# Binary cross entropy over 8192 x 8192: two large slots with split targets instead of three smaller ones with one target slot

## The chip, the cores and the metric

The kernel runs on one core of one Trainium2 chip. The metric is the device time of one execution in microseconds (us), lower is better; the median of the runs is compared. A profile is one further execution of the same program with the hardware profiler on.

## The reference

```python
def setup_inputs():
    return {
        "pred": np.random.uniform(0.01, 0.99, (8192, 8192)).astype(np.float32),
        "target": np.random.randint(0, 2, (8192, 8192)).astype(np.float32),
    }

def reference(pred, target):
    eps = 1e-7
    pred = np.clip(pred, eps, 1 - eps)
    return -(target * np.log(pred) + (1 - target) * np.log(1 - pred))
```

Targets are 0 or 1, so the result of an element is -ln(|(t - 1) + p|) with the clipped p: for t = 1 the logarithm's argument is p, for t = 0 it is 1 - p. The kernel computes it in this form. Two float32 arrays of 268.4 MB are read and one is written.

## The kernel before

The arrays are taken as one flat run of elements, cut into **chunks**. A chunk of width w takes 128 x w consecutive elements, and partition r gets row r of w elements, so a transfer has 128 rows of one contiguous run each. `plan` (lines 17 to 24) makes the list: two chunks of width FIRST (5120), then 35 of width BIG (14336), two of LAST (5632) and one of TAIL (1024), 40 in all. They are numbered k = 0 to 39; the big ones are 2 to 36, and a, b, c are the last three (37, 38, 39).

Two tiles hold everything. `ring_p` (line 53) is float32 and has SLOTS = 3 slots of BIG columns and a strip of TAIL columns for c. Predictions land in a slot, all steps work in place, and the result is stored from the same slot; chunk k of the big ones takes slot (k - 1) % 3. `ring_t` (line 54) is bfloat16 and has **one** slot of BIG columns and the strip; targets are cast from float32 to bfloat16 by the transfer that loads them.

The steps of a chunk, each a helper:

- `load_t(k)` (line 75) and `load_p(k)` (line 72) are issued by GpSimd (POOL); only chunk 0's predictions come from ScalarE's queue (line 70), as two transfers of 64 rows.
- `clip` (line 88) on VectorE (DVE): max and min with the two bounds.
- `log` is three instructions: on DVE (t - 1) + p (line 94), then on ScalarE (ACT) `Abs` (line 97) and `Ln` (line 98).
- `back` (line 102) on DVE multiplies by -1.
- `store(k)` (line 79) is issued by POOL; from k = n - 3 = 37 on by SyncE (SP). `store_rows` (line 84) stores c as three transfers on SP.

The order is written out by hand (lines 104 to 158): each engine takes its instructions in the order in which they stand there, and an instruction that waits holds up all behind it on its engine. The waits follow from the tiles: a load into a slot waits until what was there has been read, a step waits for the step before it on the same columns.

A big chunk is computed in two halves (the `h` loop, line 123): clip and log of half 0, clip and log of half 1, then back of both. On POOL's queue the order around big chunk k is `load_t(k+1)`, `store(k)`, `load_p(k+2)`. As there is one target slot, `load_t(k+1)` waits until line 94 has read the second half of chunk k's targets. `load_p(k+2)` goes into the slot of chunk k - 1 and waits for that chunk's store. In the last big chunk (the `else` at line 128) the loads of a, b and c are issued instead, and the clips of a and b stand between the two halves' backs. At the end (lines 145 to 158) DVE's order is log of both halves of a, clip of c, log of b's first half, back of a's first half, and so on, with the stores of a, b and c on SP as they come ready.

Of the kernel before, what the change touches and what calls it, by code (L numbers as in the profile page):

```python
# [1 line left out]

# [4 lines left out]

EPS = 1e-7

BIG = 14 * 1024  # L10
FIRST = 5 * 1024
LAST = 5632
TAIL = 1024
SLOTS = 3


def plan(total):
    n = (total - 2 * FIRST - 2 * LAST - TAIL) // BIG
    assert n > 4 and total == 2 * FIRST + n * BIG + 2 * LAST + TAIL
    spots = [(FIRST, 0, 0), (FIRST, FIRST, FIRST)]  # L20
    spots += [(BIG, k % SLOTS * BIG, 0) for k in range(1, n + 1)]
    end = (n + 1) % SLOTS * BIG
    spots += [(LAST, end, 0), (LAST, end + LAST, LAST)]
    return spots + [(TAIL, SLOTS * BIG, BIG)]


@with_exitstack
def kernel(
    ctx: ExitStack,
    tc: tile.TileContext,  # L30
    pred: bass.AP,
    target: bass.AP,
    out: bass.AP,
):
    nc = tc.nc
    fp32 = mybir.dt.float32
    bf16 = mybir.dt.bfloat16
    Alu = mybir.AluOpType
    Act = mybir.ActivationFunctionType
    P = nc.NUM_PARTITIONS  # L40

    R, C = pred.shape
    spots = plan(R * C // P)
    n = len(spots)
    widths = [s[0] for s in spots]
    cols = [sum(widths[:k]) for k in range(n)]

    def chunk(ap, k):
        flat = ap.rearrange("r c -> (r c)")
        return flat[cols[k] * P : (cols[k] + widths[k]) * P].rearrange("(p w) -> p w", p=P)  # L50

    pool = ctx.enter_context(tc.tile_pool(name="rings", bufs=1))
    ring_p = pool.tile([P, SLOTS * BIG + TAIL], fp32, name="ring_p", tag="ring_p")
    ring_t = pool.tile([P, BIG + TAIL], bf16, name="ring_t", tag="ring_t")
    warm = pool.tile([1, 8], fp32, name="warm", tag="warm")

    def spot(k, part=(0, 1)):
        w, c, _ = spots[k]
        i, m = part
        return ring_p[:, c + i * w // m : c + (i + 1) * w // m]  # L60

    def spot_t(k, part=(0, 1)):
        w, _, c = spots[k]
        i, m = part
        return ring_t[:, c + i * w // m : c + (i + 1) * w // m]

    def load_p(k):
        if k == 0:
            for rows in (slice(0, P, 2), slice(1, P, 2)):
                nc.scalar.dma_start(out=spot(0)[rows], in_=chunk(pred, 0)[rows])  # L70
        else:
            nc.gpsimd.dma_start(out=spot(k), in_=chunk(pred, k))  # L72

    def load_t(k):
        nc.gpsimd.dma_start(out=spot_t(k), in_=chunk(target, k))  # L75

    def store(k):
        queue = nc.sync if k >= n - 3 else nc.gpsimd
        queue.dma_start(out=chunk(out, k), in_=spot(k))  # L79

    def store_rows(k):
        src, dst = spot(k), chunk(out, k)
        for first, last in ((0, 108), (108, 120), (120, 128)):
            nc.sync.dma_start(out=dst[first:last], in_=src[first:last])

    def clip(k, *part):
        p = spot(k, *part)
        nc.vector.tensor_scalar(  # L88
            out=p, in0=p, scalar1=EPS, scalar2=1 - EPS, op0=Alu.max, op1=Alu.min
        )  # L90

    def log(k, *part):
        p = spot(k, *part)
        nc.vector.scalar_tensor_tensor(  # L94
            out=p, in0=spot_t(k, *part), scalar=1.0, in1=p, op0=Alu.subtract, op1=Alu.add
        )
        nc.scalar.activation(out=p, in_=p, func=Act.Abs)  # L97
        nc.scalar.activation(out=p, in_=p, func=Act.Ln)  # L98

    def back(k, *part):  # L100
        p = spot(k, *part)
        nc.vector.tensor_scalar(out=p, in0=p, scalar1=-1.0, scalar2=None, op0=Alu.mult)  # L102

    with tc.manual_schedule():
        nc.vector.memset(warm, 1.0)  # L105
        load_t(0)
        load_p(0)
        load_t(1)
        load_p(1)
        load_p(2)  # L110
        nc.scalar.activation(out=warm, in_=warm, func=Act.Ln)  # L111
        for k in (0, 1):
            clip(k)
            log(k)
        load_t(2)
        back(0)
        store(0)
        back(1)
        store(1)
        load_p(3)  # L120
        a, b, c = range(n - 3, n)
        for k in range(2, n - 3):
            for h in (0, 1):
                clip(k, (h, 2))
                log(k, (h, 2))
            if k < n - 4:
                load_t(k + 1)
            else:
                load_t(a)
                load_t(b)  # L130
                load_p(c)
                load_t(c)
                back(k, (0, 2))
                for j in (a, b):
                    clip(j)
            if k < n - 4:
                back(k, (0, 2))
            back(k, (1, 2))
            store(k)
            if k + 2 < n - 3:  # L140
                load_p(k + 2)
            elif k + 2 == n - 3:
                load_p(a)
                load_p(b)
        log(a, (0, 2))
        log(a, (1, 2))
        clip(c)
        log(b, (0, 2))
        back(a, (0, 2))
        log(b, (1, 2))  # L150
        back(a, (1, 2))
        store(a)
        log(c)
        back(b, (0, 2))
        back(b, (1, 2))
        store(b)
        back(c)
        store_rows(c)


# [1 line left out]
_INS = ['pred', 'target']  # L162
_OUTS = [((8192, 8192), 'float32')]


# [23 lines left out]
```

## Time and profile before

| what | value |
|---|---|
| time, median of 3 runs | 1864.76 us (1864.24 to 1865.12) |
| span of the profiled execution | 1863.3 us |
| the runs' median less that span | 1.5 us |
| DVE busy | 1121.6 us (60%), 230 instructions |
| ACT busy | 902.4 us (48%), 156 instructions |
| POOL busy | 178.7 us (10%), 120 instructions |
| DVE idle ahead of line 94, until a target load landed | 370.7 us in 35 waits |
| POOL idle ahead of line 75, until line 94 was done | 1056.4 us in 37 waits |
| POOL idle ahead of line 79, until line 102 was done | 584.2 us |
| transfers of big chunks, us from issue to landing | predictions 44.3, targets 31.3, stores 31.1 |

The profiled execution's own time outside the profile isn't recorded; the runs' median lies 1.5 us above its span, and that is taken for what lies around a span. The page divides the span into 40 slices; its DMA row is the mean busy share of the core's 16 DMA engines in tenths. The GB/s row counts bytes as they land, so that a target load that reads 4 bytes and writes 2 counts half of what it reads. Idle time of an engine that isn't the bottleneck costs nothing.

### The profile page before, as it was taken

Reading aid. Unit: us, or ns where it says so; the run is one execution under the profiler, and the core shown is the slowest. Engines: PE = TensorE matmul, PEld = TensorE weight load, DVE = VectorE, ACT = ScalarE, POOL = GpSimd, SP = SyncE. Lnnn points to the kernel's source line nnn. Section 1 sums busy time; section 2 is a strip of 40 time slices with the busy share of each in tenths; the row PEclk is TensorE's granted clock in tenths of the full one; section 3 lists DMA queues with packets and bytes.
Section 4 is the critical chain, followed back from the end, with each engine's and each line's share of the span. In section 5 each row is a group of like instructions: output and inputs, shape, how many; then the busy total and the mean of one; then the engine's idle time right before and its main releaser. Section 6 shows DMA issues by size and latency. Waiting matters only on the chain.

```text
span 1863.3 us, 713 instructions
## 1 busy us (share of the span) xinstructions
DVE 1121.6 (60%) x230; ACT 902.4 (48%) x156; POOL 178.7 (10%) x120
## 2 busy tenths in 40 slices
DVE  4666555555666566655555666566655555666565
ACT  4454444455555544444445555544444445555554
POOL 1111101111110011101111110011101111110020
DMA  9999999999999999999999999999999999999999
GB/s 344 348 370 356 355 356 355 355 355 355 357 375 374 374 372 355 355 355 355 355 355 355 359 374 374 375 375 361 355 355 356 356 356 355 356 367 374 374 353 352
DMA packets 17318, 671.15 MB, mean 360 GB/s; under 512 B 1952, under 2 KB 1952, under 8 KB 2336
## 3 DMA queue, kind: packets, MB, share of 16 engines
q0 software_dynamic: 16704, 662.18, 99.0%
q1 hardware_dynamic: 448, 6.29, 0.8%
q10 hardware_dynamic: 160, 2.62, 0.4%
q14 instruction: 6, 0.05, 0.0%
HBM read 536.87 MB, written 268.44 MB: 432 GB/s over the span
## 4 chain that ended last, share of the span: by engine, by line
DMA 60%; issue 35%; ACT 3%; DVE 1%; POOL 0%; POOLq 0%; DVEq 0%; PEldq 0%
DMA ring_t<-in_target_dram 58%; DMA ring_p<-in_pred_dram 2%; ACT ring_p L98 1%; ACT ring_p L97 1%; DVE ring_p L94 1%; DVE ring_p L102 0%; POOL out_dram L79 0%; DVE ring_p L88 0%; POOL ring_t L75 0%; POOLq L75 0%; POOL ring_p L72 0%; POOLq L79 0%; DVEq L94 0%; PEldq L184 0%
## 5 line engine op out<-in xcount | busy, mean ns | idle before, releaser
L97 ACT ACTIVATE ring_p<-ring_p 128x7168 f32<-128x7168 f32 (+3 forms) x77 | 452.0, 5870 | 940.7 <-DVE ring_p L94 940.7
L94 DVE SCALAR_TENSOR_TENSOR ring_p<-ring_t,ring_p 128x7168 f32<-128x7168 bf16 (+3 forms) x77 | 558.2, 7251 | 372.0 <-DMA ring_t<-in_target_dram 370.7
L102 DVE TENSOR_SCALAR ring_p<-ring_p 128x7168 f32<-128x7168 f32 (+3 forms) x77 | 285.4, 3707 | 329.4 <-ACT ring_p L98 329.4
L98 ACT ACTIVATE ring_p<-ring_p 128x7168 f32<-128x7168 f32 (+3 forms) x77 | 452.6, 5877 | 2.4
L88 DVE TENSOR_SCALAR ring_p<-ring_p 128x7168 f32<-128x7168 f32 (+3 forms) x75 | 284.6, 3794 | 24.4 <-DMA ring_p<-in_pred_dram 24.4
L79 POOL DMA_DIRECT2D out_dram<-ring_p x37 | 128.0, 3459 | 584.4 <-DVE ring_p L102 584.2
L75 POOL DMA_DIRECT2D ring_t<-in_target_dram x40 | 29.0, 724 | 1057.2 <-DVE ring_p L94 1056.4
L72 POOL DMA_DIRECT2D ring_p<-in_pred_dram x39 | 21.8, 561 | 2.5 <-issue 2.5
L111 ACT ACT_TABLE_LOAD x1 | 1.3, 1283 | 1.9 <-issue 1.9
L105 DVE MEMSET warm<- 1x8 f32 x1 | 0.1, 65 | 0.8 <-PEq L173 0.8
L111 ACT ACTIVATE warm<-warm 1x8 f32<-1x8 f32 x1 | 0.2, 208 | 0.0
L173 POOL MEMSET const-float32-0.0<- 128x1 f32 x1 | 0.1, 99 | 0.2 <-issue 0.2
L173 POOL MEMSET const-bfloat16-1.0<- 128x1 bf16 x1 | 0.1, 102 | 0.0
L173 POOL MEMSET const-uint8-127<- 128x1 uint8 x1 | 0.1, 100 | 0.0
L173 POOL MEMSET const-float32-1.0<- 128x1 f32 x1 | 0.1, 99 | 0.0
## 6 DMA issues: line engine op xcount, KB each, us to landing
ring_p<-in_pred_dram POOLq DMA_DIRECT2D x35, 7168.0 KB, 44.3
out_dram<-ring_p POOLq DMA_DIRECT2D x35, 7168.0 KB, 31.1
ring_t<-in_target_dram POOLq DMA_DIRECT2D x35, 3584.0 KB, 31.3
ring_p<-in_pred_dram POOLq DMA_DIRECT2D x2, 2816.0 KB, 37.1
out_dram<-ring_p SPq DMA_DIRECT2D x2, 2816.0 KB, 14.6
out_dram<-ring_p POOLq DMA_DIRECT2D x2, 2560.0 KB, 27.9
ring_t<-in_target_dram POOLq DMA_DIRECT2D x2, 1408.0 KB, 26.5
ring_p<-in_pred_dram ACTq DMA_DIRECT2D x2, 1280.0 KB, 10.5
```

The lines of the kernel that those rows point to most:

```text
L72: nc.gpsimd.dma_start(out=spot(k), in_=chunk(pred, k))
L75: nc.gpsimd.dma_start(out=spot_t(k), in_=chunk(target, k))
L79: queue.dma_start(out=chunk(out, k), in_=spot(k))
L88: nc.vector.tensor_scalar(out=p, in0=p, scalar1=EPS, scalar2=1 - EPS, op0=Alu.max, op1=Alu.min)
L94: nc.vector.scalar_tensor_tensor(out=p, in0=spot_t(k, *part), scalar=1.0, in1=p, op0=Alu.subtract, op1=Alu.add)
L97: nc.scalar.activation(out=p, in_=p, func=Act.Abs)
L98: nc.scalar.activation(out=p, in_=p, func=Act.Ln)
L102: nc.vector.tensor_scalar(out=p, in0=p, scalar1=-1.0, scalar2=None, op0=Alu.mult)
L105: nc.vector.memset(warm, 1.0)
L111: nc.scalar.activation(out=warm, in_=warm, func=Act.Ln)
L173: nc = _bacc.Bacc("TRN2", target_bir_lowering=False, num_devices=1)
```

## The change

Widths and slots: BIG goes from 14336 to 16384 columns (a row of a transfer has 64 KiB instead of 56), FIRST from 5120 to 3072, LAST from 5632 to 4608. There are two prediction slots instead of three, and `ring_t` gets two slots of its own, at the same column offsets as `ring_p`. The plan has then 36 chunks: 0 and 1 of 3072, 31 big ones (2 to 32), a and b (33, 34) of 4608 and c (35) of 1024. Big chunk k takes slot (k - 1) % 2 in both rings; a and b share slot 0.

Order: the loads of chunk k + 1 are issued ahead of the computing of chunk k, targets first. On POOL's queue it is then `store(k-1)`, `load_t(k+1)`, `load_p(k+1)`, `store(k)`. `load_p(k+1)` goes into the slot that `store(k-1)` reads and waits for its end. In the last big chunk the three target loads and then the three prediction loads of a, b and c are issued there. `load_t(2)` is issued at the start.

Pieces: a big chunk is computed in eight pieces of 2048 columns: clip and log of all eight, then back of all eight, then the one store.

End: the clips of a, b and c all stand ahead of the logs of a. Stores go to SP from k = n - 4 on, so that the last big chunk's store is issued there too.

```diff
-BIG = 14 * 1024
-FIRST = 5 * 1024
-LAST = 5632
+BIG = 16 * 1024
+FIRST = 3072
+LAST = 4608
 TAIL = 1024
-SLOTS = 3
+SLOTS = 2
+PIECES = 8
...
-    spots += [(BIG, k % SLOTS * BIG, 0) for k in range(1, n + 1)]
+    spots += [(BIG, k % SLOTS * BIG, k % SLOTS * BIG) for k in range(1, n + 1)]
     end = (n + 1) % SLOTS * BIG
-    spots += [(LAST, end, 0), (LAST, end + LAST, LAST)]
-    return spots + [(TAIL, SLOTS * BIG, BIG)]
+    spots += [(LAST, end, end), (LAST, end + LAST, end + LAST)]
+    return spots + [(TAIL, SLOTS * BIG, SLOTS * BIG)]
...
-    ring_t = pool.tile([P, BIG + TAIL], bf16, name="ring_t", tag="ring_t")
+    ring_t = pool.tile([P, SLOTS * BIG + TAIL], bf16, name="ring_t", tag="ring_t")
...
-        queue = nc.sync if k >= n - 3 else nc.gpsimd
+        queue = nc.sync if k >= n - 4 else nc.gpsimd
...
         load_t(1)
-        load_p(1)
-        load_p(2)
+        for k in (1, 2):
+            load_p(k)
+        load_t(2)
         nc.scalar.activation(out=warm, in_=warm, func=Act.Ln)
         for k in (0, 1):
             clip(k)
             log(k)
-        load_t(2)
-        back(0)
-        store(0)
-        back(1)
-        store(1)
-        load_p(3)
+        for k in (0, 1):
+            back(k)
+            store(k)
         a, b, c = range(n - 3, n)
-        for k in range(2, n - 3):
-            for h in (0, 1):
-                clip(k, (h, 2))
-                log(k, (h, 2))
-            if k < n - 4:
-                load_t(k + 1)
-            else:
-                load_t(a)
-                load_t(b)
-                load_p(c)
-                load_t(c)
-                back(k, (0, 2))
-                for j in (a, b):
-                    clip(j)
-            if k < n - 4:
-                back(k, (0, 2))
-            back(k, (1, 2))
+        m = PIECES
+        for k in range(2, a):
+            coming = (k + 1,) if k + 1 < a else (a, b, c)
+            for j in coming:
+                load_t(j)
+            for j in coming:
+                load_p(j)
+            for i in range(m):
+                clip(k, (i, m))
+                log(k, (i, m))
+            for i in range(m):
+                back(k, (i, m))
             store(k)
-            if k + 2 < n - 3:
-                load_p(k + 2)
-            elif k + 2 == n - 3:
-                load_p(a)
-                load_p(b)
+        for j in (a, b, c):
+            clip(j)
         log(a, (0, 2))
         log(a, (1, 2))
-        clip(c)
         log(b, (0, 2))
         back(a, (0, 2))
```

## The prediction

> **What bounds the kernel now.** I first read the page's slices and queues.
>
> ```profile
> DMA  9999999999999999999999999999999999999999
> q0 software_dynamic: 16704, 662.18, 99.0%
> q1 hardware_dynamic: 448, 6.29, 0.8%
> q10 hardware_dynamic: 160, 2.62, 0.4%
> HBM read 536.87 MB, written 268.44 MB: 432 GB/s over the span
> ```
>
> The 16 DMA engines are busy in every slice; q0 (POOL's queue) carries nearly all, q1 is SP's, q10 ACT's. 805.31 MB cross HBM whatever the tiling. Now the timeline around the last big chunks, for the rate in the middle.
>
> ```profile
> 1683.60 7.62 DVE L94 SCALAR_TENSOR_TENSOR ring_p<-ring_t,ring_p 128x7168 f32<-128x7168 bf16 x1 [10.73 <-DMA ring_t<-in_target_dram]
> ...
> 1734.34 7.63 DVE L94 SCALAR_TENSOR_TENSOR ring_p<-ring_t,ring_p 128x7168 f32<-128x7168 bf16 x1 [10.70 <-DMA ring_t<-in_target_dram]
> ...
> 1839.65 7.77 SPq L79 DMA_DIRECT2D out_dram<-ring_p  x2
> ```
>
> Line 94 of one chunk to line 94 of the next is 50.74 us; from 109.89 to 1785.01 it is 33 periods of 50.76. A period moves 3 x 7.34 MB = 22.02 MB: 433.8 GB/s. At that rate 805.31 MB take 1856.4 us, of a span of 1863.3. So DVE's waits for targets, and POOL's for line 94, cost nothing: behind them the DMA queue is full. Of the other 6.9 us, 2.0 are ahead of the first byte (the stretches of 1 to 2 and 2 to 3 us show 0 and 328 GB/s), about 1 to 2 come after the last, the rest is engines drifting apart early. The end has no hole either: DMA share 0.96 from 1785 to 1863. **A change of buffers can win a few us at most; it can lose any hole that it opens in the DMA row.** So I look for holes.
>
> **Durations.** From the groups by shape:
>
> ```profile
> L94 DVE SCALAR_TENSOR_TENSOR ring_p<-ring_t,ring_p 128x7168 f32<-128x7168 bf16 x70 | 533.8, 7625 | 371.9 <-DMA ring_t<-in_target_dram 370.7
> L98 ACT ACTIVATE ring_p<-ring_p 128x7168 f32<-128x7168 f32 x70 | 432.4, 6176 | 2.2
> L102 DVE TENSOR_SCALAR ring_p<-ring_p 128x7168 f32<-128x7168 f32 x70 | 272.6, 3894 | 319.6 <-ACT ring_p L98 319.6
> ...
> L94 DVE SCALAR_TENSOR_TENSOR ring_p<-ring_t,ring_p 128x1024 f32<-128x1024 bf16 x1 | 1.2, 1221 | 0.0
> L98 ACT ACTIVATE ring_p<-ring_p 128x1024 f32<-128x1024 f32 x1 | 1.1, 1057 | 0.0
> ...
> L102 DVE TENSOR_SCALAR ring_p<-ring_p 128x1024 f32<-128x1024 f32 x1 | 0.7, 694 | 0.4 <-ACT ring_p L98 0.4
> ```
>
> A line through the two widths gives, for 2048 and 2304 columns: line 94 2.29 and 2.56 us; line 98 (97 alike) 1.91 and 2.12; lines 88 and 102 1.23 and 1.36. Successive DVE instructions start about 0.08 us before the one ahead ends. Transfers at 433.8 GB/s: 16384 columns 19.34 us, 4608 columns 5.44, 3072 columns 3.63, 1024 columns 1.21.
>
> **Part 1: slots and order in the middle, 0 us.** A big chunk's period becomes 58.0 us of DMA. Compute: clip and line 94 of eight pieces are 8 x 3.46 = 27.7 us on DVE, the eight backs 8 x 1.15 = 9.2, so 36.9; ACT (3.6 + 8 x 3.75 = 33.6) is ready before the last back. With 0.4 us from landing to start (as in this trace), a store is issued 37.3 us after its predictions land. In the queue the order is store(k-1), targets k+1, predictions k+1. While chunk k is computed these three run, so store(k) must be there within 58.0 us: margin 20.7. The new wait is predictions k+1 on the end of store(k-1); behind it on POOL stand only store(k) and what follows, and the cover is targets k+1, 19.3 us. From issue to first byte took 1.33 us on ACT's queue (0.74 to 2.07) and, beside it, at most 4.6 on POOL's (1.24 to 5.82); a POOL issue took 0.53 us, up to 3.6 when it met a DVE instruction of 3.9, so with clips of 1.23 about 1.3. Six us under 19.3: no hole. If the cover were gone, each chunk would pay those 2 to 6 us, 31 times. The added fixed costs (DVE from 210 to 744 instructions on big chunks at some 0.15 us, ACT likewise) lie inside the 36.9 and so under the DMA.
>
> **Part 2: larger, fewer transfers, -0.8 us.** The trace's packet records have 2.116 us for a 56 KiB row, 0.836 for 22 KiB, 0.159 for 4 KiB: 8.4 ns a row beyond the bytes. A DMA engine takes 8 rows of each transfer; 35 x 24 rows become 31 x 24: 96 x 8.4 ns = 0.8 us less. Were a 64 KiB row split in two, it would be 744 x 8.4 = 6.2 us more. I take the first: no row is split so far.
>
> A rule of the Trainium skill speaks against this (DMA: Bandwidth & Descriptors, Latency and other measured facts): copies whose rows lie a large power of two apart slow down, to 207 GB/s at 512 KiB and 103 at 4 MiB from 214, and 64 KiB is such a distance where 56 wasn't. By 207 of 214, an estimate from that page, the sum would gain some 60 us. No big row here lies so; the one power of two, c's 4 KiB, shows only the 8.4 ns.
>
> **Part 3: the start, 0 us.** Chunks 0 and 1 are smaller, but the first byte comes as early, and the queue then holds four transfers of 3.63 us and predictions and targets 2 (19.3 each), to 55 us. Chunk 1's result is ready at about 30, so the first stores are queued in time. Targets 2 no longer wait for line 94 at 37 us, but their queue was covered to 44 anyway.
>
> **Part 4: the end, +17.9 us.** Put time 0 where chunk 32's predictions have landed. The queue of POOL then holds store(31) (19.3), the targets of a, b, c (12.1) and, from store(31)'s end on, their predictions: a 31.4 to 36.9, b to 42.3, c to 43.5. But store(32) is now on **SP's queue**, issued at 37.3, with its first row at about 38.7 to 39.3. It doesn't stand behind b and c: it runs beside them. How two queues share is in the trace twice. At the start, ACT's predictions 0 beside POOL's targets 0, the queue view from 7 to 13 us:
>
> ```profile
> q10 hardware_dynamic: 69, 1.29, 50.9%
> q0 software_dynamic: 60, 0.61, 48.4%
> ```
>
> One to one in rows. At the end, with unequal rows, the packet records of one engine read: POOL's 56 KiB row ends 1843.34, SP's 22 KiB row to 1844.17, POOL's 56 KiB row to 1846.28, then SP's again. So engines alternate **row by row, whatever the size**. At 39.3 an engine has 4 rows of b and 8 of c left. Each now waits behind a 64 KiB row (2.4 us): 8 such rows, and c's last come when all is done, at 62.9, instead of 43.5.
>
> The Trainium skill (DMA: Bandwidth & Descriptors, Queues, rings and completion order) has an engine drain a packet of some 9 to 17 rows from one ring before it switches. By that, b and c could slip through together ahead of the store and the sum would lose these 17.9 us; the records disagree, with single rows taking turns.
>
> DVE's order is now clip a, b, **c**, and only then log a. Clip c can't start until about 63.4. From there: clip c to 64.1; line 94 of a's halves and b's first to 71.6 (3 x 2.5); back of a's first half to 72.9; line 94 of b's second to 75.4; back of a's second half, whose Ln is done at 66.7 + 2 x 4.2 = 75.1, to 76.7. Store a is issued there, first byte 1.4 later at 78.1: DMA has stood empty for 15.2 us since 62.9. Store a runs to 83.5. ACT finishes b at 83.5, back to 84.9, store b's first byte at 86.2: 2.7 us empty. Then b to 91.6, c to 92.9. Without holes the three stores would end at 62.9 + 12.1 = 75.0. Loss 17.9. Nothing covers it: all loads are over.
>
> **Sum.** -0.8 + 17.9 = +17.1; 1863.3 + 17.1 = 1880.4 of span, and with the 1.5 us by which the runs' median lies above the span, **1881.9 us** (+0.9%). Its own range is 1876 to 1887: if SP splits a 64 KiB row in two, c lands some 4 us earlier; if POOL's queue does, 6.2 us come on top; compute of chunk 32 is good to 2 us either way, which moves only which rows are left.
>
> **Rivals.**
> 1. **The loads of a, b and c get through** (the other side: not slower). Place: rows of b and c left when store(32) reaches the DMA engines. If none is left, c lands at 43.5, log a starts at 44.5, store a is ready at 57, before store(32) ends at 62.9; no hole, 1863.3 - 0.8 + 1.5 = 1864.0, no change. The point: store(32) would have to arrive after 43.5, that is compute 5 us longer than 37.3, or POOL's rows be favoured. If the queues shared by bytes, c would land at 39.3 + 2 x 4.2 = 47.7; store a is ready at 62.4, b at 70.7 with 1 and 3 us of hole: about 1868. For it: small rows might be fetched ahead several at a time (POOL's first two went together at the start). Against: the turns above. Chance 0.13, about half at 1864 and half at 1868.
> 2. **The middle gets slower**: rows of 64 KiB move at a lower rate, or the wait on store(k-1) leaves a hole each time. Each 1% of the 31 x 58.0 = 1798 us is 18 us; 1% on top of the forecast is 1900. For it: the new row distance, two slots instead of three. Against: 19.3 and 20.7 us of cover, and the same rate per byte at 4, 22 and 56 KiB apart from 8 ns a row. Chance 0.08, most of it from 1888 up.
> 3. **Faster**: no hole at the end, and the start's drift of some 3 us shrinks: 1860. Against: the floor of 1856.4 + 2 + 1.5. Chance 0.03.
>
> **Chances and range.** Forecast 0.76, rivals 0.13, 0.08, 0.03. About 0.2% (3.7 us) is what a measurement of this kernel can tell from no change. Slower 0.76 + 0.08 = 0.84, same 0.13, faster 0.03. The forecast's own range holds about 0.73; I reach down to 1867 for the sharing by bytes and up to 1890 for the smallest loss in the middle: 0.81.
>
> **What would show it.** Right: line 94 of the same piece recurs every 58 us in a full DMA row; DVE waits for predictions at clip b (some 14 us) and again at clip c (6); the queue view has SP's 8 MB store landing while b and c are still under way; then a hole of about 15 us in the DMA row and a second of 3. Part 1 is wrong if the period is over 58.2 or DMA sags in mid-run; part 4 is wrong if c's clip starts before 50 us after chunk 32's landing, and then the whole loss falls away.

## The result and the profile after

The changed kernel takes **1886.92 us** (1886.53 to 1887.34, 4 runs), the kernel before, beside it, 1864.94 us. The ratio is 1.0117, 95% interval 1.0105 to 1.0129: 22.0 us slower. The profiled execution took 1886.53 us, of which 1884.7 are the span; that span is 21.4 us longer than before.

The page of the changed kernel, the same rows as before:

```profile
DMA  9999999999999999999999999999999999999994
...
q0 software_dynamic: 14832, 655.89, 97.1%
q1 hardware_dynamic: 592, 13.63, 1.7%
...
q14 instruction: 11, 0.09, 0.0%
HBM read 536.87 MB, written 268.44 MB: 427 GB/s over the span
```

The bytes are the same and the DMA row is full in 39 slices; only the last has a 4. SP's queue q1 carries 13.63 MB instead of 6.29: the last big store. Here is the end in the timeline (start, length, engine, line, idle time before it and what ended that; lines 88, 94, 97, 98 and 102 are now 89, 95, 98, 99 and 103; the SP row gathers three issues, the stores of chunk 32, a and b, of which the first is at 1827.19):

```profile
1790.28 1.23 DVE L89 TENSOR_SCALAR ring_p<-ring_p 128x2048 f32<-128x2048 f32 x1 [21.08 <-DMA ring_p<-in_pred_dram]
...
1827.19 47.82 SPq L80 DMA_DIRECT2D out_dram<-ring_p  x3
1827.34 2.56 DVE L89 TENSOR_SCALAR ring_p<-ring_p 128x4608 f32<-128x4608 f32 x1 [0.18 <-DMA ring_p<-in_pred_dram]
1840.01 2.56 DVE L89 TENSOR_SCALAR ring_p<-ring_p 128x4608 f32<-128x4608 f32 x1 [10.11 <-DMA ring_p<-in_pred_dram]
1853.28 0.69 DVE L89 TENSOR_SCALAR ring_p<-ring_p 128x1024 f32<-128x1024 f32 x1 [10.71 <-DMA ring_p<-in_pred_dram]
1853.88 7.49 DVE L95 SCALAR_TENSOR_TENSOR ring_p<-ring_t,ring_p 128x2304 f32<-128x2304 bf16 x3
...
1865.03 1.35 DVE L103 TENSOR_SCALAR ring_p<-ring_p 128x2304 f32<-128x2304 f32 x1
...
1873.29 1.36 DVE L103 TENSOR_SCALAR ring_p<-ring_p 128x2304 f32<-128x2304 f32 x1 [2.81 <-ACT ring_p L99]
```

Chunk 32's predictions were in use at 1790.28. Its store was issued 36.9 us later, and a was clipped at once. Then DVE waited 10.1 us for b and 10.7 us for c, a chunk of 1024 columns, whose clip started 63.0 us after chunk 32's. Only behind it came the logs of a, and back of a's second half ended at 1866.4. What the DMA engines did meanwhile is in the stretches (length, busy time of DVE, ACT and POOL, clock, DMA share, GB/s):

```profile
1840.00:1845.00 5.00, 2.56 (x1) 0.00 (x0) 0.00 (x0) 1.00 1.00 434
1845.00:1850.00 5.00, 0.00 (x0) 0.00 (x0) 0.00 (x0) 1.00 0.55 238
1850.00:1855.00 5.00, 1.72 (x2) 0.00 (x0) 0.00 (x0) 1.00 0.01 3
1855.00:1860.00 5.00, 5.00 (x3) 3.50 (x2) 0.00 (x0) 1.00 0.00 0
1860.00:1865.00 5.00, 5.00 (x3) 4.97 (x4) 0.00 (x0) 1.00 0.00 0
1865.00:1870.00 5.00, 3.40 (x4) 4.97 (x3) 0.00 (x0) 1.00 0.56 236
1870.00:1875.00 5.00, 1.84 (x2) 4.94 (x4) 0.00 (x0) 1.00 0.55 236
```

That is the forecast hole: from 1845 to 1870 the shares leave 0.45 + 0.99 + 1 + 1 + 0.44 of 5 us each, 19.4 us empty (15.2 were forecast; most engines run dry 4 to 5 us ahead of the last), and 2.3 more between stores a and b. A share counts a packet whole in the stretch in which it starts, so a row can be off by some tenths, and a share can exceed 1. The queue view of 1849 to 1853.5 us shows what DVE waited for (packets, MB, share):

```profile
q1 hardware_dynamic: 5, 0.07, 3.4%
q0 software_dynamic: 6, 0.02, 1.1%
```

Nearly all is over, and six packets of q0 remain: c's last five rows of 4 KiB and a record of 4 bytes behind them. In the packet records (put together by engine, each record beginning where one ended) fourteen engines ended b and c and then, from 1828.1 us on, took the store's eight rows in a block, most of them until 1847.5 to 1848.6. One engine had three rows of c left when it took its first row of the store. One more lagged by some 5 us: when it took its first row of the store, at 1831.0, it had two rows of b and all eight of c still to do, and there the rows take turns, 64 KiB of the store, 18 KiB of b, 64 KiB, and so on, until c's last row ends at 1852.9. **One late engine of sixteen sets when a load has landed.**

### The profile page after: what moved, and what is told of

Read it like the earlier page. It is cut to its first block, busy times and chain, and to the rows that moved or that the text cites. A ratio compares the mean times of both kernels' runs of the same rounds, so it can differ in the third digit from the quotient of the medians.

```text
span 1884.7 us, 1546 instructions
## 1 busy us (share of the span) xinstructions
DVE 1171.3 (62%) x764; ACT 954.8 (51%) x512; POOL 56.4 (3%) x107
## 3 DMA queue, kind: packets, MB, share of 16 engines
q1 hardware_dynamic: 592, 13.63, 1.7%
## 4 chain that ended last, share of the span: by engine, by line
DMA 38%; issue 30%; DVE 30%; ACT 1%; POOL 1%; POOLq 0%; DVEq 0%; PEldq 0%
DMA ring_p<-in_pred_dram 34%; DVE ring_p L95 15%; DVE ring_p L89 7%; DVE ring_p L103 7%; DMA out_dram<-ring_p 4%; ACT ring_p L99 1%; ACT ring_p L98 0%; POOL ring_t L76 0%; POOL out_dram L80 0%; POOL ring_p L73 0%; POOLq L80 0%; DVEq L95 0%; PEldq L174 0%; POOLq L73 0%; POOLq L76 0%
## 5 line engine op out<-in xcount | busy, mean ns | idle before, releaser
L98 ACT ACTIVATE ring_p<-ring_p 128x2048 f32<-128x2048 f32 (+2 forms) x255 | 485.1, 1902 | 910.4 <-DVE ring_p L95 910.4
L89 DVE TENSOR_SCALAR ring_p<-ring_p 128x2048 f32<-128x2048 f32 (+2 forms) x253 | 312.1, 1233 | 667.6 <-DMA ring_p<-in_pred_dram 667.6
L95 DVE SCALAR_TENSOR_TENSOR ring_p<-ring_t,ring_p 128x2048 f32<-128x2048 bf16 (+2 forms) x255 | 586.4, 2300 | 27.3 <-DMA ring_t<-in_target_dram 18.8
L99 ACT ACTIVATE ring_p<-ring_p 128x2048 f32<-128x2048 f32 (+2 forms) x255 | 489.0, 1918 | 8.1
L103 DVE TENSOR_SCALAR ring_p<-ring_p 128x2048 f32<-128x2048 f32 (+2 forms) x255 | 293.8, 1224 | 9.0 <-ACT ring_p L99 9.0
L80 POOL DMA_DIRECT2D out_dram<-ring_p x32 | 17.2, 537 | 545.6 <-DVE ring_p L103 545.6
L76 POOL DMA_DIRECT2D ring_t<-in_target_dram x36 | 19.8, 551 | 0.8 <-PEq L174 0.8
## 6 DMA issues: line engine op xcount, KB each, us to landing
ring_t<-in_target_dram POOLq DMA_DIRECT2D x2, 1152.0 KB, 47.5
```

The costliest lines, as they stand in the source:

```text
L89: nc.vector.tensor_scalar(out=p, in0=p, scalar1=EPS, scalar2=1 - EPS, op0=Alu.max, op1=Alu.min)
L95: nc.vector.scalar_tensor_tensor(out=p, in0=spot_t(k, *part), scalar=1.0, in1=p, op0=Alu.subtract, op1=Alu.add)
```

## The experiments

Theory A: the loss is at the end and has two links. The last big store on SP shares the DMA engines row by row with the loads still under way, so that c lands late; and clip c stands ahead of log a, so that DVE, then ACT, then the stores wait for it. Rival B: the end is slow for its small pieces. Rival C: the loss is in the middle. All ratios below are to the kernel before, run on the same chip.

**Store 32 back to POOL.**

```diff
-        queue = nc.sync if k >= n - 4 else nc.gpsimd
+        queue = nc.sync if k >= n - 3 else nc.gpsimd
```

> The changed kernel with one edit: the last big chunk's store goes to POOL's queue again, behind the loads of a, b and c. Theory A (the end's loss comes from that store sharing the DMA engines row by row with the loads, so that c lands late and clip c holds up log a): c lands some 44 us after chunk 32's predictions instead of 63, no hole follows, and the time falls by about 18 us, from 1886.9 to about 1869 us; what is left over the kernel before, about 4 us, is the middle and the start. Rival B (the end is slow because of its small pieces on DVE and ACT, whatever queue the store takes): the time stays within 4 us of 1886.9. Rival C (all of the loss lies in the middle): the same, no change.

Measured: 1868.88 us, ratio 1.0021 (1.0012 to 1.0030); 18.0 us of the 22.0 are gone. Its timeline:

```profile
1790.97 1.23 DVE L89 TENSOR_SCALAR ring_p<-ring_p 128x2048 f32<-128x2048 f32 x1 [21.08 <-DMA ring_p<-in_pred_dram]
...
1833.42 3.16 DVE L89 TENSOR_SCALAR ring_p<-ring_p 128x4608 f32<-128x4608 f32 x2 [2.83 <-DMA ring_p<-in_pred_dram]
1836.50 7.49 DVE L95 SCALAR_TENSOR_TENSOR ring_p<-ring_t,ring_p 128x2304 f32<-128x2304 bf16 x3
```

The clips of b and c run on end from 1833.42 and the logs of a start 45.5 us after chunk 32, where they started 63.6 after it. B and C fall as the main cause. This run has a smaller hole of its own, ahead of store 32; it comes up again below.

**Clip c ahead of log c**, store on SP.

```diff
-        for j in (a, b, c):
+        for j in (a, b):
             clip(j)
...
+        clip(c)
         log(c)
```

> The changed kernel with one edit: clip c stands right ahead of log c, behind store a, instead of ahead of log a; the store stays on SP. Theory A: c still lands some 63 us after chunk 32's predictions, but log a starts when b has landed and been clipped, 52.7 us after them in the profile, so store a is issued some 11 us earlier; the hole shrinks by about 11 to 12 us: about 1875 us. Rival B: no change. A rival in which the sharing itself, and not the wait of DVE for c, costs the time (DMA working slower with two queues): no change either.

Measured: 1875.36 us, ratio 1.0057 (1.0045 to 1.0070). Only DVE's order changed and 11.6 us came back. Back of a's second half ends at 1855.2 instead of 1866.4, 11.2 us earlier, while b landed just as late (its clip starts at 1840.26). So late landing costs through what waits behind it; the logs of a still wait behind the clip of b here, and the time is still 10.6 us over the kernel before.

**All of a, then b, then c**, store on SP.

```diff
-        for j in (a, b, c):
-            clip(j)
+        clip(a)
+        for h in (0, 1):
+            log(a, (h, 2))
+        for h in (0, 1):
+            back(a, (h, 2))
+        store(a)
+        clip(b)
...
+        clip(c)
+        log(c)
+        for h in (0, 1):
+            back(b, (h, 2))
```

> The changed kernel with DVE's order at the end written so that nothing of a waits for b or c: clip, log and back of a and its store, then clip and log of b, clip and log of c, back and store of b, back and store of c; the big store stays on SP beside the loads. Theory A: store a is issued before the big store ends, one short hole of 3 to 4 us ahead of store b remains; about 1868 us. By the theory that sharing the DMA engines costs time in itself: above 1880 us.

Measured: 1872.17 us, ratio 1.0039 (1.0026 to 1.0052): well under 1880, so sharing in itself isn't the price, but 4 us over what theory A gave. I had still left back b behind clip c; the timeline and, below it, the stretches show it:

```profile
1854.77 0.69 DVE L89 TENSOR_SCALAR ring_p<-ring_p 128x1024 f32<-128x1024 f32 x1 [5.50 <-DMA ring_p<-in_pred_dram]
```

```profile
1850.00:1855.00 5.00, 0.23 (x1) 4.97 (x3) 0.00 (x0) 1.00 0.49 211
1855.00:1860.00 5.00, 4.83 (x5) 2.39 (x3) 0.00 (x0) 1.00 0.08 33
```

DVE waits 5.5 us for c, until 1854.77. ACT had b's first half ready at 1851.1 and its second at 1855.3, but back of the second half ends only at 1859.3, some 2.5 us later than it could without c ahead of it. The hole ahead of store b is 2.6 + 4.6 = 7 us instead of 3 to 4; so clip c's place explains some 2.5 of the 4 us, and the rest stays open.

**The store in rows of 8 KiB.** Eight stores on SP, each behind its own back.

```diff
             for i in range(m):
                 back(k, (i, m))
-            store(k)
+                if k + 1 == a:
+                    w = widths[k] // m
+                    nc.sync.dma_start(out=chunk(out, k)[:, i * w : (i + 1) * w], in_=spot(k, (i, m)))
+            if k + 1 < a:
+                store(k)
```

> The changed kernel, but the last big chunk's store goes out on SP as eight stores of 2048 columns, each behind its own back, so with rows of 8 KiB instead of 64 KiB. Theory A with turns row by row: a row of the loads now waits behind 0.31 us and not 2.4 us; the 24 rows of a, b and c an engine has are held up by some 7 us in all, c lands about 51 us after chunk 32's predictions instead of 63, and the time falls by about 12 us to about 1875 us. If the queues shared by bytes: c lands at about 55 us, and the gain is about 8 us, 1879 us. If c's late landing were no matter of row size: 1887 us, no change.

Measured: 1874.37 us, ratio 1.0052 (1.0038 to 1.0066). The three clips:

```profile
1829.41 2.56 DVE L89 TENSOR_SCALAR ring_p<-ring_p 128x4608 f32<-128x4608 f32 x1 [2.29 <-DMA ring_p<-in_pred_dram]
1837.26 2.56 DVE L89 TENSOR_SCALAR ring_p<-ring_p 128x4608 f32<-128x4608 f32 x1 [5.29 <-DMA ring_p<-in_pred_dram]
1840.95 0.69 DVE L89 TENSOR_SCALAR ring_p<-ring_p 128x1024 f32<-128x1024 f32 x1 [1.13 <-DMA ring_p<-in_pred_dram]
```

Chunk 32 starts at 1790.24 here, so c is in use 50.7 us after it, where turns by rows gave 51 and sharing by bytes 55. All engines take turns of 18 KiB and 8 KiB in the records. The eight stores also begin 8 us earlier (1819.20), which by itself would hold the loads up more, not less. So row size sets the share.

**The kernel before, with only its last big store on SP.**

```diff
-        queue = nc.sync if k >= n - 3 else nc.gpsimd
+        queue = nc.sync if k >= n - 4 else nc.gpsimd
```

> The kernel before (three slots, 56 KiB rows, halves) with one edit: the last big chunk's store goes to SP's queue (k >= n - 4). Its loads of c are still on their way when that store is issued at 1822.4 us. Theory A (rows of the two queues take turns, the slowest DMA engine's last rows of c wait behind eight rows of the store): c lands at about 1844 instead of 1829 us, clip c, which stands ahead of log b and back a, waits some 14 us, and a hole of 8 to 10 us opens ahead of store a: about 1873 to 1875 us. If it needs the changed kernel's slots or pieces for the loss: 1865 us, no change.

Measured: 1876.50 us, ratio 1.0063 (1.0050 to 1.0076), 12.0 us slower by one queue; somewhat more than forecast.

```profile
1822.42 40.50 SPq L79 DMA_DIRECT2D out_dram<-ring_p  x3
...
1847.01 0.69 DVE L88 TENSOR_SCALAR ring_p<-ring_p 128x1024 f32<-128x1024 f32 x1 [18.62 <-DMA ring_p<-in_pred_dram]
```

In the kernel before, the same clip stood at 1829.85, after a wait of 1.7 us; now DVE waits 18.6:

```profile
1829.85 0.69 DVE L88 TENSOR_SCALAR ring_p<-ring_p 128x1024 f32<-128x1024 f32 x1 [1.70 <-DMA ring_p<-in_pred_dram]
```

Neither slots nor pieces are needed for the loss.

**The same with clip c and log c behind store b.**

```diff
-        clip(c)
         log(b, (0, 2))
...
-        log(c)
         back(b, (0, 2))
         back(b, (1, 2))
         store(b)
+        clip(c)
+        log(c)
```

> The kernel before with its last big store on SP (1876.5 us with that alone), and with clip c and log c moved behind store b. Theory A: c still lands near 1847 us, but nothing of a and b waits for it; stores a and b are issued at about 1839.6 and 1847 us, before the store ahead of them has ended, so no hole opens: 1864 to 1866 us, the kernel before's time, and sharing the DMA engines between two queues costs nothing by itself. If sharing costs: 1868 us or more.

Measured: 1866.65 us, ratio 1.0007 (0.9998 to 1.0016): about 10 of the 12 us are back, 0.7 us over the range I gave, and not told apart from the kernel before. Its profiled span is 1863.5 against 1863.3. No hole is left: the five stretches of 5 us from 1830 to 1855 have DMA shares of 0.93, 1.22, 0.77, 1.05 and 1.01, together 4.98 of 5. If sharing costs anything by itself it is under 3 us (0.0016 of the time).

**What the other 4 us are.** With store 32 on POOL the time, 1868.88, is still 4.1 us over the kernel before. Three more kernels, all with the store on POOL. First, widths as before (BIG 14336, FIRST 5120, LAST 5632), eight pieces:

> The changed kernel with the big store on POOL (its end's loss is away, 1868.9 us), and the widths of the kernel before: BIG 14336, FIRST 5120, LAST 5632, so rows of 56 KiB in two slots, eight pieces of 1792. The question is the 4 us that are left over the kernel before, which show as periods of 58.3 to 58.8 us instead of 57.95 in the first 700 us. Theory M1 (the 64 KiB rows, with their distance, cost it): about 1865 to 1866 us, the first periods like the later ones. Theory M2 (two slots and the new order in the queue cost it, whatever the row): 1869 us or a little more, and the first periods 0.3 to 0.5 us over the later ones.

Measured: 1873.23 us, ratio 1.0046 (1.0034 to 1.0059). Inconclusive as a time: with a wider a and a shorter last store a hole came back ahead of store a (DMA share 0.08 from 1845 to 1850). The first periods read 51.25, 50.78, 50.80, 50.99, 50.94, then 50.71 to 50.82: nearer to the kernel before (51.10, 50.73, 50.78, 51.10, 50.66) than to 64 KiB rows.

Then pieces: four, and sixteen (`PIECES = 4`, `PIECES = 16`).

> The changed kernel with the big store on POOL, with four pieces of 4096 columns instead of eight. Theory M3 (the many instructions cost the 4 us: their fetches ride on the DMA engines, and their work beside the transfers): about half the instructions on big chunks, so some 2 us less, about 1867 us. Theories M1 and M2: no change, 1868.9 us.

> The changed kernel with the big store on POOL and sixteen pieces of 1024 columns. Theory M3 (instruction fetches: a packet of 8 KiB on a DMA engine, 0.67 us of lag whenever it falls on the slowest one): four pieces took 1866.8 us, eight 1868.9; sixteen have about twice the fetches of eight, so 3 to 4 us more, 1872 to 1873 us, with more periods at 58.6 instead of 57.95. If pieces don't matter: 1868.9.

Measured: four pieces 1866.78 us, ratio 1.0013 (1.0004 to 1.0022); sixteen 1872.39 us, 1.0041 (1.0027 to 1.0055). So 4, 8 and 16 pieces take 1866.8, 1868.9 and 1872.4 us, with this row for the queue that fetches instructions (packets), four, eight and sixteen pieces in turn:

```profile
q14 instruction: 6, 0.05, 0.0%
```

```profile
q14 instruction: 11, 0.09, 0.0%
```

```profile
q14 instruction: 21, 0.17, 0.0%
```

With eight pieces four of the later periods are 58.64 instead of 57.95 us, and in the packet records each has a fetch of 8 KiB (0.31 us) early in it, for instance at 1039.92; the row of 64 KiB that starts as it ends took 2.79 us instead of 2.42. Together that is some 0.67 us, when it falls on the engine that sets the pace:

```profile
1035.47 1.23 DVE L89 TENSOR_SCALAR ring_p<-ring_p 128x2048 f32<-128x2048 f32 x1 [21.09 <-DMA ring_p<-in_pred_dram]
1094.10 1.23 DVE L89 TENSOR_SCALAR ring_p<-ring_p 128x2048 f32<-128x2048 f32 x1 [21.75 <-DMA ring_p<-in_pred_dram]
1152.06 1.23 DVE L89 TENSOR_SCALAR ring_p<-ring_p 128x2048 f32<-128x2048 f32 x1 [21.08 <-DMA ring_p<-in_pred_dram]
```

DVE's wait for predictions is 21.75 us there and 21.08 beside it: DMA was late, not DVE. Other fetches leave no mark. So about 2 of the 4 us go with the doubled number of pieces (shown by the dose).

Where they are lost is another question: a longer period says that the slowest of the sixteen engines was late, not that the others stood still. The packet records tell how many bytes were still to move at 1820 us (targets at the 4 bytes an element that are read), here as time at 433.8 GB/s, one profiled execution each:

| kernel | span, us | transfers left at 1820 us | span left | lost behind 1820 us |
|---|---|---|---|---|
| before | 1863.3 | 40.1 | 43.3 | 3.2 |
| changed | 1884.7 | 40.4 | 64.7 | 24.3 |
| store on POOL, four pieces | 1865.3 | 40.9 | 45.3 | 4.4 |
| store on POOL, eight pieces | 1867.5 | 40.3 | 47.5 | 7.2 |
| store on POOL, sixteen pieces | 1870.4 | 40.7 | 50.4 | 9.7 |
| store on POOL, 56 KiB rows, eight pieces | 1871.5 | 40.3 | 51.5 | 11.2 |

At 1820 us all are level to within 0.9 us, and four pieces are no better off than eight. So the 4 us of eight pieces over the kernel before are lost at the end (7.2 against 3.2), most of them ahead of store 32. On POOL's queue that store stands behind the loads of a, b and c and is issued when chunk 32 is done, at 1826.83, 1828.14 and 1833.44 us with four, eight and sixteen pieces; its first rows start at 1829.70, 1831.28 and 1836.30. By then most engines have run out of loads, with eight pieces by 1828.4, though the last one has some until 1834.3. The stretches from 1825 to 1835, for four, eight and sixteen pieces in turn:

```profile
1825.00:1830.00 5.00, 4.01 (x2) 0.00 (x0) 2.29 (x1) 1.00 1.18 501
1830.00:1835.00 5.00, 3.81 (x3) 0.00 (x0) 0.00 (x0) 1.00 1.06 456
```

```profile
1825.00:1830.00 5.00, 4.81 (x4) 0.00 (x0) 1.86 (x1) 1.00 0.68 287
1830.00:1835.00 5.00, 2.17 (x2) 0.00 (x0) 0.71 (x1) 1.00 1.00 431
```

```profile
1825.00:1830.00 5.00, 5.00 (x9) 3.20 (x4) 0.00 (x0) 1.00 0.69 293
1830.00:1835.00 5.00, 5.00 (x7) 0.00 (x0) 1.56 (x1) 1.00 0.11 45
```

Chunk 32's first clip moves with the pieces too: 1788.70, 1790.97 and 1793.61. With sixteen pieces the computing up to the store's issue is also longer, 39.8 us against 37.2. That more fetches make the last engine later, and through it chunk 32 and its store, fits these rows and the four periods; no run changes the fetches alone, so it isn't shown.

Next, 56 KiB rows again, four pieces, and the end's order a, b, c:

> Widths of the kernel before (56 KiB rows), two slots, four pieces, the last big store on POOL, and at the end a done and stored before b is touched, b before c. The eight-piece run with these widths had a hole of some 5 us ahead of store a (1873.2 us) and two periods of 51.4 us beside instruction fetches. If those two are what it lost beside the first periods, about 1866 us is left; if the two slots cost time by themselves in the middle, 1868 us or more. Beating the kernel before (1864.5) is expected by no theory.

Measured: 1872.83 us, ratio 1.0042 (1.0030 to 1.0055), against the 1866 hoped for. A fault of my order: a went first, b's clip and log stood behind back a, and the hole moved ahead of store b (DMA share 0.47 from 1850 to 1855, 0.00 to 1860). As a time it says nothing of the middle.

Last, the distance of the rows. Four pieces, rows of 64 KiB either 1984 KiB apart or 2 MiB apart (all chunks):

```diff
+        if 2 <= k < n - 3:
+            bigs = flat[cols[2] * P : cols[n - 3] * P].rearrange("(p w) -> p w", p=P)
+            return bigs[:, (k - 2) * BIG : (k - 1) * BIG]
```

```diff
-        return flat[cols[k] * P : (cols[k] + widths[k]) * P].rearrange("(p w) -> p w", p=P)
+        return flat.rearrange("(p w) -> p w", p=P)[:, cols[k] : cols[k] + widths[k]]
```

> Four pieces, the big store on POOL (1866.8 us), and the big chunks take other elements of the arrays: row r of all of them lies in one run, so the 64 KiB rows of a transfer lie 1984 KiB apart (31 x 64) instead of 64; each element is still computed once. If the distance of 64 KiB, a power of two, costs the first periods their 0.1 to 0.7 us: about 1865 us, first periods at 57.95. If the distance is no matter: 1866.8 us.

> The same, with all chunks cut from 128 runs of 2 MiB, so that the rows of each transfer lie 2 MiB apart, a larger power of two. If such a distance slows the transfers, it is seen in every period of 58 us; if not, 1866.8 us. By the Trainium skill (DMA: Bandwidth & Descriptors, Latency and other measured facts: 164 GB/s of 214 at 2 MiB) the middle of 1797 us would take some 550 us more, an estimate from that page, about 2400 us.

Measured: 1984 KiB 1867.00 us, ratio 1.0012 (1.0003 to 1.0021), as with 64 KiB, and the first periods are as long (58.06 to 58.71). So 64 KiB being a power of two is not what lengthens them. 2 MiB: 1910.45 us (1904.40 to 1916.58), ratio 1.0244 (1.0222 to 1.0266), 43.7 us over the four pieces at 64 KiB. Some periods go up to 60.8 us, others stay at 57.95. The start loses some 15 us of it: line 95 of chunk 2 begins at 65.22 us instead of 57.56, and the first period is 55.67 instead of 48.70. The Trainium skill's rule (DMA: Bandwidth & Descriptors, Latency and other measured facts), measured there for copies of 16 KiB rows on the sync and scalar queues, holds here in its direction at 2 MiB, with a loss of 2.3%, not the quarter that its 164 of 214 GB/s would make.

## Why the prediction was right

The time, 1886.9 us, lay 5.0 above the 1881.9 forecast and inside the range, on the upper edge of the forecast's own 1876 to 1887.

- **Part 4, the end (+17.9).** Right in mechanism, 3.2 us short in size. Behind 1820 us the changed kernel lost 24.3 us and the kernel before 3.2: 21.1 us, for 17.9 forecast, because most engines were done with the store 4 to 5 us before the last one had c, so that the holes were longer (19.4 and 2.3 us, for 15.2 and 2.7). That undoing the one link, store 32's queue, gave back 18.0 us, nearly the 17.9, is partly chance: that run has a hole of its own ahead of the store (at 1840 us it has 23.0 us of transfers left, the kernel before 20.2). The times in between came as worked out; the forecast counts them from the landing of chunk 32, some 0.4 us ahead of its first clip. From that clip, computing took 36.9 us to the store's issue (36.9 forecast), c's clip came after 63.0 us (63.0), back a's second half ended after 76.1 (76.3), and there were two holes, as forecast. One picture was off: I had all engines take turns, with four rows of b and eight of c left. Fourteen ended both first; DVE waited for the one that lagged, with two rows of b left. That is also why b came sooner than forecast (49.7 us, a wait of 10.1 instead of 14) and c's wait was longer (10.7 instead of 6). The loss still came, because a load lands with its last row. That one engine would lie so far behind wasn't in the working, so luck had a part in it.
- **Part 1, the middle (0).** The order and the two slots left no hole: the DMA row is full, the later periods are 57.95, for 58.0 forecast, and at 1820 us the changed kernel is 0.3 us behind the kernel before. The added fixed cost of the pieces is hidden there, as forecast. It isn't hidden at the end when store 32 stands on POOL's queue; the instruction fetches, which ride on the engines that are the bound, had no term at all. About 2 us lie between eight pieces and four.
- **Part 2 (-0.8).** Rows of 64 KiB go as one packet each (2.418 us in the records). The saving is too small to be seen alone.
- **Part 3, the start (0).** The first ten periods of the run with the store on POOL add up to some 3.3 us above 57.95, the kernel before's to some 1 us above 50.74. These are the delays of the slowest engine; the bytes moved by 1820 us differ by 0.2 us, so part 3's zero holds. What makes the engines drift apart isn't the distance of the rows. With 56 KiB rows in two slots the sums are 1.2 and, in the run with four pieces, 2.1 us; whether row size or chance makes the rest stays open.
- **The 5.0 us above the forecast** are then 3.2 from part 4, 1.1 from what lies ahead of 1820 us (0.3, for -0.8 forecast), and 0.7 from what lies around a span (the runs' median is 2.2 us above it, for 1.5).
- **Rivals.** Rival 1's condition was met on fourteen engines of sixteen: their loads got through. Two had loads left, and that was enough. The middle, rival 2, did not get slower beyond those 0.3 us.

No version beat the kernel before. The best of the changed kernel, four pieces with the store on POOL, is 2.3 us over its neighbour run.

## What to carry to other kernels

In a kernel whose DMA row is full, ask of each edit whether it can open a hole, above all at the end, where no load is left to fill it. A large store put on a second queue doesn't wait behind the loads already queued: it takes turns with them row by row, and the smaller rows lose; so either keep it in the same queue, or let nothing urgent wait in an engine's order for a small, late transfer. A full DMA row hides that one engine is late; at the end the others run dry while work still waits for it. Look for an instruction that waits for the last transfer and stands ahead of work that is already fed: here moving one clip was worth 11 us.

## What the runs showed of the hardware that I had not expected

- Instruction fetches are DMA traffic: 6, 11 and 21 packets of 8 KiB for 4, 8 and 16 pieces; beside four of the eleven a period was some 0.67 us longer.
- The sixteen DMA engines drift apart within one queue, and a landing is that of the last: with the store on POOL they end the same loads between 1827.7 and 1834.3 us.
- Rows 2 MiB apart cost 2.3% here, unevenly (60.8 us in some periods, 57.95 in others); 1984 KiB apart cost nothing against 64 KiB.
